# Reordering the products of the feed-forward units of a two-layer encoder trunk: g7 and g4 ahead of the down products, another opening of unit 1

## The chip, the cores and the metric

The kernel runs on one core of one Trainium2 chip. The metric is the device time of one execution in microseconds (us); lower is better. The engines are called as in the profile: PE (matrix products; PEld its weight loads), DVE (vector), ACT (scalar and activation), POOL (general purpose) and SP, which issues DMA transfers. POOL issues transfers too, among them those that add what they bring to what is in the buffer.

## What is computed

Two layers over a sequence of 512 positions with 1024 features. Layer 0 mixes the positions with a gated linear recurrence, layer 1 with stick-breaking attention; each mixer is followed by a gated feed-forward block of 2816 inner features. Everything is float32.

```python
def reference(x, norm_mix_g, norm_ffn_g, ...):
    for layer in range(DEPTH):                       # 2 layers
        h = _rmsnorm(x, norm_mix_g[layer])
        mix = _rglru_mixer(...) if layer % 2 == 0 else _sb_mixer(...)
        x = x + mix
        h = _rmsnorm(x, norm_ffn_g[layer])
        x = x + _swiglu(h, ffn_w_gate[layer], ffn_w_up[layer], ffn_w_down[layer])
    return _rmsnorm(x, final_g)

def _swiglu(h, w_gate, w_up, w_down):
    g = h @ w_gate.astype(h.dtype)
    u = h @ w_up.astype(h.dtype)
    return (jax.nn.silu(g) * u) @ w_down.astype(h.dtype)
```

The change touches the two feed-forward blocks and the final norm.

## The kernel before

**Split products.** Each float32 operand is split into a high half (`wh`, a cast on ACT) and a low half (`wl`, the difference, on DVE or POOL; line L302). A product is three matmuls: high times high, high times low, low times high (L760 to L762). So every weight block of 128x1024, called a chunk here, costs PE 12 matmuls of 512 columns, ACT one cast and DVE or POOL one subtraction.

**Units.** The 2816 inner features are worked in five full units of 512 and one half unit of 256 (`NU` = 5; units 0 to 5). A two-by-two block scheme with seven products instead of eight is used twice: for gate and up (steps g1 to g7, two chunks each in a full unit, c0 and c1) and for the down product of the previous unit (steps d1 to d7, one chunk each). Unit 0 has no down products. `tt` transposes the previous unit's activations on PE; o1 and o2 make the operands of the down products out of them on ACT and DVE; q1 and q2 multiply up by silu of gate on DVE.

**Weights of the products.** Sums of weight blocks are built up in place. g1 and g2 use raw blocks. g5 uses the sum of two blocks in a buffer `bu`: SP loads one, POOL adds the other with an accumulating transfer (L90). When g5's chunk has been split, POOL adds a third block to the same buffer, which makes g6's weights, and after g6 a fourth, which makes g4's. g3 uses a raw block in a buffer `bv`; when that has been split, POOL adds a block, which makes g7's weights. The sums of down weights are made on POOL (`minus`, L142) and DVE (`sums`, L162).

**Banks.** The eight PSUM banks are used in pairs: A, B, `db` and `tb`. In a unit, A takes g1, then g6 on top (copied out to `u2`), then g7 (added to `b5`), then g4, which after silu is gate's second half; then g2 overwrites A. B takes g5 and g3. q2 and q1 read A. The down products use `db` and `tb`, and after each one DVE adds the banks to the result rows `y`.

**What sets the order.** In the feed-forward blocks the order on PE, ACT, DVE and POOL is that of the program text: a string per unit lists the steps. A product's `chunk()` also issues the casts and subtractions of the chunk three places ahead; there are four buffers for split weights, so the cast of a chunk can run once the chunk four places ahead of it in the list has been multiplied. SP issues loads up to some ten chunks ahead. Each engine works through its list in order and waits at the first entry that is not ready.

Of the kernel before, what the change touches and what calls it, by code (L numbers as in the profile page):

```python
# [17 lines left out]
S = 512  # L18
# [14 lines left out]
NU = 5  # L33
# [11 lines left out]
class Unit:  # L45
    def __init__(self, kern, l, u):
        self.kern, self.u = kern, u
        self.w = FB if u < NU else FB // 2
        self.np = 2 if u < NU else 1
        self.kt = 2 if u < NU else 4  # L50
        self.src = kern.a["w_gu"][l, 8 * u:8 * u + 4 * self.np]
        self.down = kern.a["w_dn"][l, 4 * (u - 1):4 * u] if u else None
        self.b, self.d = {}, {}
        self.direct = u == NU
        if u == 0:
            self.order = "g1 g5 stats g2 x0 g6 x1 g3 q1 g4 x2 g7 x3"
        elif u < NU:
            self.order = "g5 g1 tt g6 o1 o2 g3 d1 d2 g7 d6 d5 g4 d7 d3 g2 d4"
        else:
            self.order = "g5 g1 tt g6 o1 g3 o2 d1 g2 d2 g7 d6 d5 g4 q2 d7 tn d3 d4"  # L60
        if u == NU - 1:
            self.order = self.order.replace("g2 d4", "g2 q1 d4")
        self.pieces = []
        for n in self.order.split():
            if n[0] not in "gd":
                continue
            q = int(n[1])
            self.pieces += [Piece(self, q, c) for c in range(self.np)] if n[0] == "g" else [DownPiece(self, q)]


class Piece:
    LOADS = {1: ("raw", 0), 2: ("raw", 2), 5: ("bu", 0), 3: ("bv", 3)}
    HOME = {1: 1, 2: 2, 5: 5, 6: 5, 4: 5, 3: 3, 7: 3}
    def __init__(self, unit, q, c):
        self.unit, self.q, self.c = unit, q, c
        self.pool = (q, c) in ((7, 1), (2, 1)) and unit.u > 0 and unit.np == 2
        self.summed = False

    def buf(self, tag, pool, bufs):
# [51 lines left out]
class DownPiece(Piece):  # L131
    def __init__(self, unit, q):
        self.unit, self.q, self.c = unit, q, 0
        self.pool = q in (5, 4)
        self.summed = False

    def ready(self):
# [6 lines left out]
    def load(self):  # L144
        un, kern = self.unit, self.unit.kern
        for k in {1: ("12", "22", "11"), 2: ("21",)}.get(self.q, ()):
            t = un.d[k] = kern.raw_buf() if k in ("11", "21") else self.buf("d" + k, kern.fp, 1)
            kern.nc.sync.dma_start(t, un.down[("11", "21", "12", "22").index(k)])
        if self.q == 1:
            un.d["t"] = self.buf("dt", kern.fp, 1)  # L150
            n = 6 if un.direct else 3
            self.minus("t", "22", "12", n)
            self.minus("12", "12", "11", n + 1)

# [14 lines left out]
class Kern:  # L169
# [318 lines left out]
    def finish(self, banks, ys, g):  # L488
# [2 lines left out]
        nc.vector.tensor_scalar(g, g, -0.5, None, ALU.mult)  # L491
        row = lambda i, lo, hi: st[:, NT * i + lo:NT * i + hi]
        sq = [self.tmp() for _ in range(2)]
        late = ((1, 1), (2, 1), (3, 1))

        def gather(t, h):
            y = ys[t][:, hs[h]]
# [5 lines left out]
        def half(t):  # L503
            nc.vector.tensor_scalar(row(2, t, t + 1), row(0, t, t + 1), 1.0 / D, EPS, ALU.mult, ALU.add)

        def root(t):
            nc.scalar.activation(row(3, t, t + 1), row(1, t, t + 1), AF.Sqrt, scale=1.0 / D, bias=row(2, t, t + 1))

        def chain(lo, hi):
            s1, v0, r, v, q = (row(i, lo, hi) for i in (1, 2, 3, 4, 5))  # L510
            nc.vector.scalar_tensor_tensor(v, s1, 1.0 / D, v0, ALU.mult, ALU.add)
            nc.vector.reciprocal(r, r)
            nc.vector.tensor_tensor(v, v, r, ALU.mult)
            nc.vector.tensor_tensor(v, v, r, ALU.mult)
            nc.vector.scalar_tensor_tensor(q, v, -3.0, r, ALU.add, ALU.mult)
# [26 lines left out]
        gather(3, 0)  # L542
        store(1, 1)
        store(0, 1)
        chain(2, 3)
        gather(3, 1)
        half(3)
        root(3)
        store(2, 1)
        store(1, 0)  # L550
        store(2, 0)
        chain(3, 4)
        store(3, 0, 2)
        store(3, 1, 2)

    def v_chunk(self, pv, c):
# [167 lines left out]
    def ffn(self, l, gnext):  # L724
# [3 lines left out]
        with tc.tile_pool(name=f"ffn{l}", bufs=1) as self.fp, \  # L728
# [67 lines left out]
            def dproduct(q, two, mid):  # L796
                wh, wl = self.chunk()
                n, first, a, d = DOWN[q]
                banks = two[n]
                for i in range(2):  # L800
                    for p in range(2):
                        mm3(banks[i], *stat(q, p, i), wh[:, ts(p, S)], wl[:, ts(p, S)], first and p == 0, p == 1)
                if mid:
                    mid()
                for i in range(2):
                    t = 2 * a + i
                    o = y[t][:, ts(d, S)]
                    if gnext and (t, d) not in started:
                        started.add((t, d))
                        nc.scalar.copy(o, banks[i])  # L810
                    else:
                        add(o, o, banks[i])
# [9 lines left out]
            for u in range(NU + 1):  # L822
                un = self.unit_of()
                w = un.w
                A, B = gb
                B2 = tb if u == 0 else B if u == NU else A
                B4 = db if u == 0 else A
                two = (tb, db) if u == NU else (db, tb)
# [107 lines left out]
                        split([t[:, p] for t in hn], A[p])  # L936

                steps = dict(q1=q1, q2=q2, g1=g1, g2=g2, g3=g3, g4=g4, g5=g5, g6=g6, g7=g7, stats=stats, tt=tt, o1=o1, o2=o2, tn=tn)
                mids = {7: q2, 4: q1} if u < NU - 1 else {7: q2} if u < NU else {2: q1}
                steps.update({f"d{q}": (lambda q=q: dproduct(q, two, mids.get(q))) for q in range(1, 8)})  # L940
                steps.update({f"x{t}": (lambda t=t: None if gnext else turned(t)) for t in range(NT)})
                for n in un.order.split():
# [440 lines left out]
```

## Time and profile before

| what | value |
|---|---|
| median of 3 runs | 1137.63 us (1136.78 to 1137.96) |
| profiled execution, its own time | 1136.93 us |
| span of the profiled execution | 1135.2 us |
| granted PE clock, mean | 0.995 |
| feed-forward units 1 to 5 of layer 0 | 206 to 493 us of the span |
| feed-forward units 1 to 5 of layer 1 | 824 to 1114 us |
| last matmul starts | 1125.03 us |

Rows of the timeline have: start in us from the span's start, duration, engine, line, operation, output and inputs, shapes, and in brackets how long the engine was idle before it and what ended that. `x2` merges two like operations in a row; the duration is then that of both. Rows of waits have: who waited for whom, us in total, times, longest. Rows of transfers have: what was issued by which queue, how many, size, median us from issue to landing. In the prediction, lines are those of the kernel before; in the change everything behind the first edit stands two lines further down.

### The profile page before, as it was taken

What the parts mean: (1) busy time and instruction counts of PE and PEld (TensorE: products, weight loads), DVE (VectorE), ACT (ScalarE), POOL (GpSimd) and SP (SyncE); (2) the same over time, 40 slices, a digit from 0 to 9 for tenths busy, and PEclk for the clock granted to TensorE, in tenths of its full rate; (3) what the DMA queues carried; (4) which work ended last, traced back from release to release, by engine and by line L of the source; (5) the groups of instructions that cost most, each with busy time, mean ns of one, the idle gap of its engine ahead of it and who ended that gap; (6) DMA issues with size and microseconds to landing.
All of it is one profiled execution on the core that took longest, in us unless ns stands there. A gap on an engine that the chain in (4) does not pass through costs nothing.

```text
span 1135.2 us, 14824 instructions
## 1 busy us (share of the span) xinstructions
PE 1098.4 (97%) x5265; PEld 908.2 (80%) x5265; DVE 893.1 (79%) x1237; ACT 708.0 (62%) x1088; POOL 415.0 (37%) x271
## 2 busy tenths in 40 slices
PE   9999999999999999899999999899999999999986
PEld 6887788788888888778888888778878887888865
DVE  7878887686969687987388898768478796969797
ACT  6598567565545464535389999868574655555454
POOL 2451232335353534214044443412135344353422
PEclk9999999999999999999999999999999999999998
DMA  8522338858485857242334333125876858584511
GB/s 284 163 79 89 111 116 218 174 159 203 139 205 126 236 113 222 64 155 81 102 103 110 96 94 92 59 93 151 200 150 182 182 159 192 154 204 115 139 48 74
DMA packets 48970, 159.87 MB, mean 141 GB/s; under 512 B 6017, under 2 KB 7553, under 8 KB 48897
## 3 DMA queue, kind: packets, MB, share of 16 engines
q1 hardware_dynamic: 36512, 113.84, 29.2%
q0 software_dynamic: 12384, 45.09, 22.5%
q8 instruction: 41, 0.67, 0.2%
q14 instruction: 33, 0.26, 0.1%
HBM read 148.43 MB, written 2.10 MB: 133 GB/s over the span
## 4 chain that ended last, share of the span: by engine, by line
PE 60%; DVE 12%; issue 7%; ACT 6%; DMA 6%; POOL 1%; SPq 0%; ACTq 0%; DVEq 0%; POOLq 0%
PE bank L761 12%; PE bank L760 12%; PE bank L762 12%; PE bank L347 6%; PE bank L349 5%; PE bank L348 5%; DMA bu<-w_gu 5%; DVE wl L302 4%; PE bank L1165 3%; ACT wh L301 2%; PE bank L1191 2%; PE bank L767 1%; DVE y L752 1%; PE bank L1110 1%; PE bank L1111 1%
## 5 line engine op out<-in xcount | busy, mean ns | idle before, releaser
L301 ACT CAST wh<-raw 128x1024 fp32r<-128x1024 f32 (+1 forms) x144 | 144.7, 1011 | 80.7 <-DVE raw L162 35.4
L760 PE MATMUL bank<-wh,ow 128*128 128x512 f32 (+1 forms) x480 | 180.2, 375 | 0.4 <-DVE u L752 0.4
L761 PE MATMUL bank<-wl,ow 128*128 128x512 f32 (+1 forms) x480 | 178.8, 372 | 0.8 <-DVE wl L302 0.8
L762 PE MATMUL bank<-wh,ow 128*128 128x512 f32 (+1 forms) x480 | 178.6, 372 | 0.0
L302 DVE TENSOR_TENSOR wl<-raw,wh 128x1024 fp32r<-128x1024 f32 (+1 forms) x110 | 142.6, 1298 | 35.9 <-ACT wh L301 34.8
L302 DVE TENSOR_TENSOR wl<-bu,wh 128x1024 fp32r<-128x1024 f32 x66 | 98.8, 1507 | 63.1 <-ACT wh L301 62.1
L90 POOL DMA_DIRECT2D bu<-w_gu x64 | 56.0, 875 | 201.0 <-DVE wl L302 140.8
L301 ACT CAST wh<-bu 128x1024 fp32r<-128x1024 f32 x66 | 69.4, 1051 | 85.6 <-DMA bu<-w_gu 55.3
L302 POOL TENSOR_TENSOR wl<-raw,wh 128x1024 fp32r<-128x1024 f32 (+1 forms) x34 | 80.1, 2355 | 115.7 <-ACT wh L301 115.7
L752 DVE TENSOR_TENSOR y<-y,bank 128x512 f32<-128x512 f32 x140 | 90.9, 679 | 18.5 <-PE bank L762 18.4
L761 PEld LDWEIGHTS bank<-wl,ow 128*128 128x128 f32 x480 | 90.5, 189 | 16.8 <-DVE wl L302 1.6
L347 PE MATMUL bank<-uh,wh 128*128 128x512 f32 x256 | 102.6, 401 | 1.4 <-DVE t L1075 0.6
L760 PEld LDWEIGHTS bank<-wh,ow 128*128 128x128 f32 x480 | 90.5, 188 | 16.8 <-DVE u L752 1.3
L762 PEld LDWEIGHTS bank<-wh,ow 128*128 128x128 f32 x480 | 90.4, 188 | 15.6
L349 PE MATMUL bank<-uh,wl 128*128 128x512 f32 x256 | 100.4, 393 | 1.4 <-DVE wl L302 1.4
L348 PE MATMUL bank<-ul,wh 128*128 128x512 f32 x256 | 99.8, 390 | 0.3 <-DVE ul L404 0.3
L761 PE MATMUL bank<-wl,hth 128*128 128x512 f32 x192 | 75.3, 392 | 3.5 <-POOL wl L302 3.1
L302 POOL TENSOR_TENSOR wl<-d,wh 128x1024 fp32r<-128x1024 f32 x20 | 50.6, 2530 | 67.7 <-ACT wh L301 67.7
L760 PE MATMUL bank<-wh,hth 128*128 128x512 f32 x192 | 75.1, 391 | 0.0
L762 PE MATMUL bank<-wh,htl 128*128 128x512 f32 x192 | 74.9, 390 | 0.0
L1133 POOL TENSOR_TENSOR spl<-t,sph 128x512 fp32r<-128x512 f32 (+1 forms) x32 | 36.3, 1157 | 85.6 <-DVE sph L1132 79.8
L459 POOL TENSOR_TENSOR acc<-acc,t 128x512 f32<-128x512 f32 x20 | 28.8, 1440 | 82.5 <-ACT t L457 75.4
(257 smaller groups left out, 2850.7 us busy)
## 6 DMA issues: line engine op xcount, KB each, us to landing
bu<-w_gu POOLq DMA_DIRECT2D x64, 512.0 KB, 6.3
raw<-w_gu SPq DMA_DIRECT2D x44, 512.0 KB, 3.5
raw<-w_dn SPq DMA_DIRECT2D x24, 512.0 KB, 6.4
bu<-w_gu SPq DMA_DIRECT2D x22, 512.0 KB, 5.5
bv<-w_gu SPq DMA_DIRECT2D x22, 512.0 KB, 3.8
bv<-w_gu POOLq DMA_DIRECT2D x22, 512.0 KB, 6.5
d<-w_dn SPq DMA_DIRECT2D x20, 512.0 KB, 5.3
raw<-w_qk SPq DMA_DIRECT2D x16, 512.0 KB, 3.5
```

Source lines behind the costliest of these rows:

```text
L90: kern.soon(lambda: kern.nc.gpsimd.dma_start(t, self.part(n), accum_op=ALU.add))
L301: self.nc.scalar.copy(wh[:, c], raw[:, c])
L302: self.wl_engine(i).tensor_tensor(wl[:, c], raw[:, c], wh[:, c].bitcast(F32), ALU.subtract)
L347: mm(out, lhsT=wh, rhs=xh, start=first, stop=False)
L348: mm(out, lhsT=wh, rhs=xl, start=False, stop=False)
L349: mm(out, lhsT=wl, rhs=xh, start=False, stop=last)
L752: add = lambda o, a, b: nc.vector.tensor_tensor(o, a, b, ALU.add)
L760: mm(out, lhsT=xh, rhs=wh, start=first, stop=False, skip_group_check=True)
L761: mm(out, lhsT=xh, rhs=wl, start=False, stop=False, skip_group_check=True)
L762: mm(out, lhsT=xl, rhs=wh, start=False, stop=last, skip_group_check=True)
L1133: nc.gpsimd.tensor_tensor(sl[:, w], sp[:, w], sh[:, w].bitcast(F32), ALU.subtract)
L1165: mm(zt[kt][:, o0:o0 + ZW[j]], lhsT=tri if j == kt else one_n, rhs=s_, start=False, stop=True, skip_group_check=True)
```

## The change

In units 1 to 4 the step string puts g7 directly behind g3, g4 behind d2 and g2 ahead of d7; d7, d3 and d4 close the unit. q2 now runs in d6 and q1 in d7 (in unit 4, q1 follows g2). Unit 1 opens with g1 instead of g5. From unit 1 on the pairs A and B are swapped. POOL takes the low halves of g7's second chunk and, in full units, of d5, d7 and d4; DVE takes that of g2's second chunk and all of unit 5's. Two subtractions on POOL are issued after one chunk instead of three. In d1 the four groups of matmuls go by weight half first. In the final norm, the row tile (3, 0) is multiplied by the gain on DVE at its store instead of on POOL, its store is one transfer instead of two, and a chain of small operations moves behind the last add.

```diff
-            self.order = "g5 g1 tt g6 o1 o2 g3 d1 d2 g7 d6 d5 g4 d7 d3 g2 d4"
+            self.order = "g5 g1 tt g6 o1 o2 g3 g7 d1 d2 g4 d6 d5 g2 d7 d3 d4"
...
         if u == NU - 1:
-            self.order = self.order.replace("g2 d4", "g2 q1 d4")
+            self.order = self.order.replace("g2 d7", "g2 q1 d7")
+        if u == 1:
+            self.order = self.order.replace("g5 g1", "g1 g5")
...
-        self.pool = (q, c) in ((7, 1), (2, 1)) and unit.u > 0 and unit.np == 2
+        self.pool = (q, c) == (7, 1) and unit.u > 0 and unit.np == 2
...
-        self.pool = q in (5, 4)
+        self.pool = q in (5, 7, 4) and not unit.direct
...
-            n = 6 if un.direct else 3
+            n = 6 if un.direct else 1
...
-        late = ((1, 1), (2, 1), (3, 1))
+        late = ((1, 1), (2, 1), (3, 0), (3, 1))
...
-        chain(2, 3)
         gather(3, 1)
         half(3)
+        chain(2, 3)
         root(3)
...
-        store(3, 0, 2)
+        store(3, 0)
...
-                for i in range(2):
-                    for p in range(2):
-                        mm3(banks[i], *stat(q, p, i), wh[:, ts(p, S)], wl[:, ts(p, S)], first and p == 0, p == 1)
+                pairs = [(i, p) for i in range(2) for p in range(2)]
+                for i, p in sorted(pairs, key=lambda e: e[1]) if q == 1 else pairs:
+                    mm3(banks[i], *stat(q, p, i), wh[:, ts(p, S)], wl[:, ts(p, S)], first and p == 0, p == 1)
...
-                A, B = gb
+                A, B = gb[::-1] if u else gb
...
-                mids = {7: q2, 4: q1} if u < NU - 1 else {7: q2} if u < NU else {2: q1}
+                mids = {6: q2, 7: q1} if u < NU - 1 else {6: q2} if u < NU else {2: q1}
```

ACT in unit 2 of layer 0, from the end of `tt`'s operand work to behind that of o2, before: `raw` of number 213 and 215 are the weights of d1 and d2, the two `bv` those of g3's second chunk (first row) and g7's two chunks (last rows).

```order
L301 CAST wh70_2378<-bv_210_2190 128x1024
L301 CAST wh71_2395<-raw213_2214 128x1024
L869 COPY u20_1495<-bank0_70 128x512
L869 COPY u21_1496<-bank1_71 128x512
L771 COPY t219_2413<-bank4_74 128x512
L756 CAST hah_1503<-t219_2413 128x256
L756 CAST hbh_1505<-bank5_75 128x512
L756 CAST hth_1507<-t220_2417 128x512
L756 CAST hth_1507<-t221_2418 128x512
L301 CAST wh472_2429<-raw215_2234 128x1024
L301 CAST wh73_2445<-bv_209_2168 128x1024
L301 CAST wh74_2465<-bv_210_2190 128x1024
```

The same place of the change:

```order
L303 CAST wh70_2378<-bv_210_2188 128x1024
L303 CAST wh71_2395<-bv_209_2170 128x1024
L871 COPY u20_1495<-bank2_72 128x512
L871 COPY u21_1496<-bank3_73 128x512
L773 COPY t220_2415<-bank4_74 128x512
L758 CAST hah_1503<-t220_2415 128x256
L758 CAST hbh_1505<-bank5_75 128x512
L758 CAST hth_1507<-t221_2419 128x512
L758 CAST hth_1507<-t222_2420 128x512
L303 CAST wh472_2431<-bv_210_2188 128x1024
L303 CAST wh73_2449<-raw213_2254 128x1024
L303 CAST wh74_2467<-raw215_2275 128x1024
```

g7's two casts stand where those of d1 and d2 stood: the first ahead of the operand work of o1 and o2, the second behind it.

DVE at the end of unit 2, before: the splits of `bu` are those of g5 of unit 3, that of `raw226` is g1 of unit 3, the adds onto `bank0` and `bank1` belong to g2, `u2` to q1, the adds onto `y` to the down products.

```order
L752 TENSOR_TENSOR y1_1500<-y1_1500,bank7_77 128x512
L302 TENSOR_TENSOR wl484_2662<-bu_224_2525,wh484_2661 128x1024
L302 TENSOR_TENSOR wl85_2686<-bu_225_2546,wh85_2685 128x1024
L752 TENSOR_TENSOR bank0_70<-r10_1493,bank0_70 128x512
L752 TENSOR_TENSOR bank1_71<-r11_1494,bank1_71 128x512
L302 TENSOR_TENSOR wl86_2709<-raw226_2548,wh86_2708 128x1024
L859 SCALAR_TENSOR_TENSOR u20_1495<-u20_1495,nrs_130,bank0_70 128x512
L859 SCALAR_TENSOR_TENSOR u21_1496<-u21_1496,nrs_130,bank1_71 128x512
L752 TENSOR_TENSOR y2_1501<-y2_1501,bank4_74 128x512
L752 TENSOR_TENSOR y3_1502<-y3_1502,bank5_75 128x512
```

The same place of the change, where `bank2` and `bank3` are A:

```order
L754 TENSOR_TENSOR bank2_72<-r10_1493,bank2_72 128x512
L754 TENSOR_TENSOR bank3_73<-r11_1494,bank3_73 128x512
L304 TENSOR_TENSOR wl484_2662<-bu_224_2505,wh484_2661 128x1024
L861 SCALAR_TENSOR_TENSOR u20_1495<-u20_1495,nrs_130,bank2_72 128x512
L861 SCALAR_TENSOR_TENSOR u21_1496<-u21_1496,nrs_130,bank3_73 128x512
L754 TENSOR_TENSOR y2_1501<-y2_1501,bank4_74 128x512
L754 TENSOR_TENSOR y3_1502<-y3_1502,bank5_75 128x512
L304 TENSOR_TENSOR wl85_2683<-bu_225_2527,wh85_2682 128x1024
L754 TENSOR_TENSOR y0_1499<-y0_1499,bank6_76 128x512
L754 TENSOR_TENSOR y1_1500<-y1_1500,bank7_77 128x512
L304 TENSOR_TENSOR wl86_2702<-raw226_2548,wh86_2701 128x1024
```

g2's adds moved ahead of both of unit 3's splits, q1 behind the first, and d7's and d3's adds onto `y` now follow q1.

POOL in the middle of unit 2, before: `bv` is g7's second chunk, `d12` the weights of d5 and later d4, `raw` g2's second chunk, `bu` of number 224 and 225 the buffers of unit 3's g5.

```order
L302 TENSOR_TENSOR wl74_2466<-bv_210_2190,wh74_2465 128x1024
L302 TENSOR_TENSOR wl476_2505<-d12_211_2210,wh476_2504 128x1024
L142 TENSOR_TENSOR d12_211_2210<-raw215_2234,raw213_2214 128x1024
L90 DMA bu_224_2525<-w_gu 128x1024
L90 DMA bu_225_2546<-w_gu 128x1024
L302 TENSOR_TENSOR wl82_2620<-raw223_2469,wh82_2619 128x1024
L302 TENSOR_TENSOR wl83_2642<-d12_211_2210,wh83_2641 128x1024
```

The same place of the change, where `dt` is the weight sum of d7:

```order
L304 TENSOR_TENSOR wl472_2432<-bv_210_2188,wh472_2431 128x1024
L92 DMA bu_224_2505<-w_gu 128x1024
L92 DMA bu_225_2527<-w_gu 128x1024
L304 TENSOR_TENSOR wl78_2545<-d12_211_2250,wh78_2544 128x1024
L144 TENSOR_TENSOR d12_211_2250<-raw215_2275,raw213_2254 128x1024
L304 TENSOR_TENSOR wl81_2604<-dt_214_2256,wh81_2603 128x1024
L304 TENSOR_TENSOR wl83_2640<-d12_211_2250,wh83_2639 128x1024
```

The two transfers for unit 3 moved ahead of d5's split.

## The prediction

> **What bounds the kernel now.** I read the busy table first, then who TensorE (PE) waited for, then the timeline of the four helper engines around one unit.
>
> ```profile
> PE 1098.4 (97%) x5265; PEld 908.2 (80%) x5265; DVE 893.1 (79%) x1237; ACT 708.0 (62%) x1088; POOL 415.0 (37%) x271
> ...
> PE bank L760 <- ACT hah L756: 4.1, 2, 2.6
> PE bank L760 <- DVE u L859: 3.3, 4, 1.6
> PE bank L761 <- POOL wl L302: 3.1, 2, 1.6
> PE bank L761 <- DVE wl L302: 3.1, 5, 1.0
> ...
> PE bank L767 <- DVE b L911: 2.3, 2, 1.2
> ```
>
> PE is busy for 97% of the span; each row behind gives the waits for one releaser: total, times, longest. The change keeps every matmul, so it can gain only what PE waits for in the feed-forward layers, plus the tail behind the last matmul. It can lose wherever a weight comes later than its product. A wait costs about 0.16 us more than its idle time, since matmuls start 0.227 us apart and are counted as 0.39 long:
>
> ```profile
> 267.81 0.39 PE L760 MATMUL bank<-wh,ow 128*128 128x512 f32 x1
> ...
> 291.35 0.39 PE L760 MATMUL bank<-wh,hah 128*128 128x512 f32 x1
> ...
> 294.06 0.39 PE L760 MATMUL bank<-wh,hbh 128*128 128x512 f32 x1
> 294.29 0.39 PE L761 MATMUL bank<-wl,hbh 128*128 128x512 f32 x1
> ```
>
> These rows are unit 2 of layer 0: its start, its d1 and its d2 (first and second matmul). A chunk of 12 matmuls takes 2.72 us, and PE did not wait once between these rows. In the new order g7 stands where d1 and d2 stand, so g7's second chunk must have its high half at 294.06 and its low half (`wl`) at 294.29, 26.48 after the unit's start. The feeders at that place, ACT and then POOL:
>
> ```profile
> 283.87 1.05 ACT L301 CAST wh<-bv 128x1024 fp32r<-128x1024 f32 x1
> 284.82 1.05 ACT L301 CAST wh<-raw 128x1024 fp32r<-128x1024 f32 x1
> ...
> 291.23 1.05 ACT L301 CAST wh<-raw 128x1024 fp32r<-128x1024 f32 x1
> 292.19 2.00 ACT L301 CAST wh<-bv 128x1024 fp32r<-128x1024 f32 x2
> ...
> 279.08 0.89 POOL L90 DMA_DIRECT2D bv<-w_gu  x1
> 286.53 0.87 POOL L90 DMA_DIRECT2D bv<-w_gu  x1 [6.56 <-DVE wl L302]
> 294.27 2.66 POOL L302 TENSOR_TENSOR wl<-bv,wh 128x1024 fp32r<-128x1024 f32 x1 [6.87 <-ACT wh L301]
> ```
>
> The casts at 283.87 (g3's second chunk) and 284.82 (d1) stand ahead of the operand work o1 and o2 on ACT, the cast at 291.23 (d2) behind it, 6.41 after the one at 284.82. The two POOL transfers at 279.08 and 286.53 add another weight block into g3's buffers and so make g7's weights. Their times to landing, one view for each (then the third transfer ahead of them, for its 5.7):
>
> ```profile
> bv<-w_gu POOLq DMA_DIRECT2D x1, 512.0 KB, 9.4
> ...
> bv<-w_gu POOLq DMA_DIRECT2D x1, 512.0 KB, 5.6
> ...
> bu<-w_gu POOLq DMA_DIRECT2D x1, 512.0 KB, 5.7
> ```
>
> So g7's first chunk was complete at 279.08 + 9.4 = 288.5 (it queued behind two others; alone it takes 5.6 to 5.7), the second at 286.53 + 5.6 = 292.1. Before, g7 was used at 296.79 and this was early enough.
>
> **The change, part by part.**
>
> *g7 directly behind g3, units 2 to 4.* The cast of g7's first chunk moves into the place of 284.82 and that of the second into the place of 291.23. First chunk: its transfer is issued when g6's and g3's splits are done. Those splits stand behind work that the new order puts ahead of the unit's start (two adds of 1.29 together and q1):
>
> ```profile
> 267.13 1.29 DVE L752 TENSOR_TENSOR bank<-r,bank 128x512 f32<-128x512 f32 x2
> ...
> 271.88 1.39 DVE L859 SCALAR_TENSOR_TENSOR u<-u,nrs,bank 128x512 f32<-128x512 f32 x2
> ...
> 275.24 2.35 DVE L302 TENSOR_TENSOR wl<-bu,wh 128x1024 fp32r<-128x1024 f32 x2
> ```
>
> I take 1.29 + 1.39 = 2.7 off: landing at 285.8, cast at 285.9, and the in-order ACT reaches the second chunk 6.41 later, at 292.3. The second chunk's own transfer hangs on the split of g3's second chunk, which does not move: 292.1. Both say 292.2. Then cast 1.05, hand-over 0.08, POOL split 2.66: 296.0, against 294.29: a wait of 1.7 in each unit. Floor: if nothing but ACT's order binds, 291.23 + 3.79 = 295.0, a wait of 0.7. Ceiling: if the first transfer still lands at 288.5, the cast is at 295.0 and the wait 4.5. I take 1.7, since two independent paths give it. Units 2 to 4 of two layers: 6 x 1.7 = 10.2. Cast and split of g7's second chunk are cover for nothing else; d1 and d2 behind it are ready.
>
> The split that decides here stays on POOL. [...]
>
> *Unit 1 opened by g1, banks swapped.* What it removes:
>
> ```profile
> 203.54 1.05 ACT L301 CAST wh<-bu 128x1024 fp32r<-128x1024 f32 x1 [5.86 <-DMA bu<-w_gu]
> ...
> 204.62 1.22 DVE L302 TENSOR_TENSOR wl<-bu,wh 128x1024 fp32r<-128x1024 f32 x1 [5.69 <-ACT wh L301]
> 213.35 1.40 DVE L911 SCALAR_TENSOR_TENSOR b<-b,nrs,bank 128x512 f32<-128x512 f32 x2
> ...
> 205.97 0.39 PE L760 MATMUL bank<-wh,ow 128*128 128x512 f32 x1
> 209.97 0.50 PE L761 MATMUL bank<-wl,ow 128*128 128x512 f32 x1 [0.76 <-DVE wl L302]
> 212.99 0.47 PE L760 MATMUL bank<-wh,a 128*128 128x512 f32 x1 [0.22 <-ACT bank L887]
> 217.17 0.50 PE L761 MATMUL bank<-wl,a 128*128 128x512 f32 x1 [0.95 <-DVE wl L302]
> ```
>
> ACT stood for 5.86 us behind g5's late transfer, and PE paid three waits, 2.7 us by the distances of matmul starts (1.9 in layer 1). g1 needs no transfer of that kind and g5 comes 5.44 later: I take all 4.6 as gained. The swap keeps the first product on banks 2 and 3, which were free, so it costs nothing. But g6's weights are g5's plus a transfer, and now there are two chunks between them, not four. Unit 1 starts at 205.97. g5's first split at 204.6 to 205.8, four adds (2 x 1.28), q2 (1.40), second split 1.22: 211.0. Transfer 5.7: 216.8. Cast 1.05, split 1.22: 219.2. Next transfer 5.7: 225.0. g3's transfer is issued at 220.5 behind it: alone it lands at 226.1, with as much queueing as in the 9.4 above at 229.9; the one ahead of it is nearly through, so I take 227.5. g7's first chunk is cast at 227.6, the second 6.41 later at 234.0, its split ends at 234.0 + 3.79 = 237.8. PE wants it at 205.97 + 26.48 = 232.45: 5.3. Layer 1 in the same way: 4.7. Together 10.0, with 7.2 as the floor (g3's transfers unqueued, 1.4 less each) and 14.8 if it lands as late as before.
>
> *q1 early, d7 d3 d4 last.* q1's four waits go: 3.3 idle plus 4 x 0.16, about 4.1 with one refill, gained, since d3, d4 and g5 now lie between q1 and the g1 that overwrites its bank. Late next: d4 writes the banks that d7's evacuation still reads, and that evacuation stands on DVE behind g5's first split and q1. The silu between them:
>
> ```profile
> 267.85 1.26 ACT L855 ACTIVATE bank<-bank,rsT 128x512 f32<-128x512 f32 x2 [1.90 <-DVE bank L752]
> ```
>
> From the end of g2: hand-over 0.2, add 0.65, silu 0.65, cast 1.05, split 1.23, q1 1.39, first add 0.69 make 5.8; d4 comes after 5.44. With the refill 0.45 in units 1 to 3: 2.7 (0 to 5). Next-unit g5 weights are loaded two chunks earlier and don't bind there.
>
> *POOL's other work.* d7 goes to POOL, g2's second chunk to DVE. POOL now issues the next unit's two transfers ahead of d5's split; each waits for a load that follows g4's splits. d5 then has about 1 us to spare once PE has waited at g7. I cost it at 0 (0 to +4 over both layers). The two subtractions come out two chunks earlier in the program but still behind the same transfers on POOL: 0.
>
> *Unit 5.* d5's split goes from POOL to DVE:
>
> ```profile
> 474.34 1.28 DVE L752 TENSOR_TENSOR y<-y,bank 128x512 f32<-128x512 f32 x2
> 475.82 2.55 DVE L302 TENSOR_TENSOR wl<-bu,wh 128x1024 fp32r<-128x1024 f32 x1 [0.21 <-ACT wh L301]
> ...
> 474.93 2.36 POOL L302 TENSOR_TENSOR wl<-d,wh 128x1024 fp32r<-128x1024 f32 x1 [19.73 <-ACT wh L301]
> ...
> 477.35 0.51 PE L761 MATMUL bank<-wl,hth 128*128 128x512 f32 x1 [1.58 <-POOL wl L302]
> ```
>
> On DVE it ends near 475.6 + 1.22 = 476.8 instead of 477.3: 0.45 a layer. In d1, ordering by weight half moves the late operand three matmuls, 0.68, and DVE is relieved of q1 at the unit's start; of 4.1 waited there I take 2.1. Together 3.0 (1 to 5.5).
>
> *Tail.* POOL no longer multiplies the last row tile's first half, and a DVE chain moves behind the last add:
>
> ```profile
> 1125.62 1.26 POOL L501 TENSOR_TENSOR y<-y,raw 128x512 f32<-128x512 f32 x1 [1.43 <-ACT t L499]
> ...
> 1125.63 1.27 DVE L513 TENSOR_TENSOR st<-st 128x1 f32<-128x1 f32 x1
> ...
> 1127.20 0.68 DVE L498 TENSOR_TENSOR y<-y,bank 128x512 f32<-128x512 f32 x1
> 1128.88 2.12 ACT L523 ACTIVATE y<-y,st 128x512 f32<-128x512 f32 x4
> ```
>
> A 128x1 operation that takes 0.16 elsewhere took 1.27 beside POOL's, and held up the last add. That add can now come at about 1125.5; the results are ready at about 1130.4 instead of 1131.0, and the stores queue less: 1.5 gained (0.4 to 2). [...]
>
> Sum: +10.2 +10.0 +2.7 -4.6 -4.1 -3.0 -1.5 = +9.7. The profiled execution took 1136.93 (span 1135.2), 0.70 under the median 1137.63; 1136.93 + 9.7 = 1146.6, as a median 1147.3; I say 1147.
>
> **The rivals.** (1) Faster: g7 waits only for ACT's order. It needs both accumulating transfers to land by 291.2, that is the second 0.9 sooner. Then 6 x 0.7 + 7.2 - 4.6 - 4.1 - 5.5 - 2 = -4.8: 1133. For it: POOL is otherwise idle there. Against it: the split that releases the second transfer sits behind tt's operand work, unmoved. It decides where the mean wait at g7 is under about 1.6. (2) A wash: the g7 wait is 1.0 in units 2 to 4, unit 1's at its floor and d4's nil: 6.0 + 7.2 - 13.2, about 1137.5. (3) Much slower: the transfers land as late as before: 6 x 4.5 + 14.8 + 2.7 - 13.2 = +31, 1169. Against it: DVE is relieved at the unit's start.
>
> **How the numbers follow.** Forecast 0.69, (1) 0.13, (2) 0.10, (3) 0.08. Less than 0.2% (2.3 us) is about what a measurement here can't tell from no change. Slower 0.69 + 0.08 = 0.77, same 0.10, faster 0.13. The forecast's own range is 1140 to 1156: waits of 1.2 to 2.4 at g7, 4 to 6 in unit 1, 0 to 5 at d4. The range 1135 to 1157 adds the wash and half of (1), and leaves out the rest of (1), most of (3) and the upper edge.
>
> **What would show it.** In the changed profile PE's waits for POOL's `wl` should grow from 3.1 in two to about 20 in eight to ten, all at g7's second chunk, the longest in unit 1; its waits for q1 (`u`, 3.3) should be gone; ACT should stand still for a `bv` transfer ahead of o1, which it did not before; d4's first matmul should wait for a DVE add on `y` up to 0.5 in units 1 to 3; the last store should be issued about 1.5 sooner after the last matmul. No POOL wait at g7 would make the prediction wrong as a whole.

## The result, and the profile after

The changed kernel took 1168.83 us (median; 1167.37 to 1172.12) against 1137.20 us of the kernel before in the same session: 1.0286 times as long, with an interval of 1.0259 to 1.0313. It is slower, as forecast, but by 32 us and not by 10; the forecast range (1135 to 1157) does not hold it. Its profiled execution took 1172.12 us with a span of 1170.4 us, 35.2 us longer than that of before. The medians of the kernel before lie between 1131.03 and 1137.20 us on the chips used, so experiments below are compared by their ratio to the kernel before on the same chip.

The busy table of the changed kernel:

```profile
PE 1114.0 (95%) x5265; PEld 916.6 (78%) x5265; DVE 911.0 (78%) x1242; ACT 711.3 (61%) x1086; POOL 400.0 (34%) x266
```

PE has the same 5265 matmuls, but is counted busy for 15.6 us longer: matmuls themselves have become slower somewhere. Its waits (who waited for whom, us in total, times, longest):

```profile
PE bank L763 <- POOL wl L304: 15.4, 8, 1.9
PE bank L762 <- ACT wh L303: 10.7, 8, 2.3
PE bank L762 <- DVE y L754: 5.8, 8, 2.1
...
PE bank L762 <- DVE u L754: 1.8, 2, 0.9
...
PE bank L762 <- ACT hah L758: 1.3, 2, 0.7
...
PE bank L762 <- DVE b L913: 0.6, 2, 0.4
...
PE bank L769 <- DVE b L913: 0.6, 2, 0.3
```

The first row is the split of g7's second chunk on POOL, once in each of units 1 to 4 of both layers; the second is for the most part the cast of the same chunk. The waits for q1 (`u`, L861 now) are gone. The place in unit 4 of layer 0, on PE (the last four rows are in d1, which follows g7's second chunk):

```profile
429.64 0.50 PE L762 MATMUL bank<-wh,s 128*128 128x512 f32 x1 [2.20 <-ACT wh L303]
432.08 0.80 PE L763 MATMUL bank<-wl,s 128*128 128x512 f32 x1 [1.94 <-POOL wl L304]
432.67 0.63 PE L764 MATMUL bank<-wh,s 128*128 128x512 f32 x1
433.10 0.63 PE L762 MATMUL bank<-wh,s 128*128 128x512 f32 x1
...
437.36 0.56 PE L763 MATMUL bank<-wl,hah 128*128 128x512 f32 x1
437.76 0.39 PE L764 MATMUL bank<-wh,hal 128*128 128x512 f32 x1
437.99 0.39 PE L762 MATMUL bank<-wh,hah 128*128 128x512 f32 x1
438.22 0.40 PE L763 MATMUL bank<-wl,hah 128*128 128x512 f32 x1
```

PE stands for 2.2 us for the high half, runs one matmul, stands for 1.94 us for the low half, and then the matmuls start 0.43 us apart instead of 0.227 until 437.8. The view by stretches names the reason (stretch, length, then busy time and count of PE, PEld, DVE, ACT and POOL, the granted PE clock, DMA share, GB/s):

```profile
432.00:437.90 5.90, 5.82 (x14) 4.65 (x15) 5.86 (x7) 1.10 (x2) 0.02 (x1) 0.52 0.31 101
437.90:443.80 5.90, 5.90 (x28) 4.86 (x27) 5.50 (x7) 2.20 (x3) 0.88 (x1) 1.00 0.71 196
```

At a clock of 0.52, 14 matmuls run in the time that 28 take at 1.00. This stretch alone costs 2.7 us on top of the waits.

How much longer each unit got, from the starts of its first matmul and of the next unit's in the two profiles, in us:

| layer | unit 1 | unit 2 | unit 3 | unit 4 | unit 5 |
|---|---|---|---|---|---|
| 0 | +5.9 | +3.8 | +5.0 | +7.2 | -0.6 |
| 1 | +5.1 | +3.0 | +3.5 | +5.5 | -2.5 |

Why the chunk comes late, in unit 3 of layer 0 (its first matmul starts at 336.41), on ACT, POOL and DVE:

```profile
344.77 1.05 ACT L303 CAST wh<-bv 128x1024 fp32r<-128x1024 f32 x1 [1.66 <-PE bank L764]
...
356.63 1.05 ACT L303 CAST wh<-bv 128x1024 fp32r<-128x1024 f32 x1 [3.10 <-DMA bv<-w_gu]
...
363.05 1.04 ACT L303 CAST wh<-bv 128x1024 fp32r<-128x1024 f32 x1
...
344.91 1.88 POOL L92 DMA_DIRECT2D bu<-w_gu  x2 [2.71 <-DVE wl L304]
347.44 0.88 POOL L92 DMA_DIRECT2D bv<-w_gu  x1 [0.65 <-DVE wl L304]
...
364.18 2.35 POOL L304 TENSOR_TENSOR wl<-bv,wh 128x1024 fp32r<-128x1024 f32 x1 [8.16 <-ACT wh L303]
...
345.86 1.23 DVE L304 TENSOR_TENSOR wl<-bv,wh 128x1024 fp32r<-128x1024 f32 x1 [0.30 <-ACT wh L303]
```

The chain: the cast of g3's first chunk (344.77) waits for PE to free a buffer; its split on DVE (the last row) stands 0.30 us for that cast and then lets POOL issue the transfer at 347.44, 11.03 us after the unit's start, behind two transfers issued at 344.9 and 345.9. ACT stands 3.10 us for it, until 356.6, 9.1 us after its issue. The cast of g7's second chunk follows 6.42 us later, behind the operand work of o1 and o2, and POOL's split ends at 366.5. PE needed it 26.48 after the unit's start, at 362.9; with the 1.5 us that PE had waited for the cast it lost 3.7 us there and 1.4 more at the low clock.

### The profile page after: what moved, and what is told of

Read it like the earlier page. It is cut to its first block, busy times and chain, and to the rows that moved or that the text cites. A ratio compares the mean times of both kernels' runs of the same rounds, so it can differ in the third digit from the quotient of the medians.

```text
span 1170.4 us, 14792 instructions
## 1 busy us (share of the span) xinstructions
PE 1114.0 (95%) x5265; PEld 916.6 (78%) x5265; DVE 911.0 (78%) x1242; ACT 711.3 (61%) x1086; POOL 400.0 (34%) x266
## 5 line engine op out<-in xcount | busy, mean ns | idle before, releaser
L304 DVE TENSOR_TENSOR wl<-raw,wh 128x1024 fp32r<-128x1024 f32 (+1 forms) x118 | 197.7, 1679 | 59.6 <-ACT wh L303 59.1
L304 DVE TENSOR_TENSOR wl<-bu,wh 128x1024 fp32r<-128x1024 f32 x66 | 82.0, 1249 | 32.2 <-ACT wh L303 31.2
L763 PEld LDWEIGHTS bank<-wl,ow 128*128 128x128 f32 x480 | 90.5, 188 | 15.4
L304 POOL TENSOR_TENSOR wl<-raw,wh 128x1024 fp32r<-128x1024 f32 (+1 forms) x26 | 59.2, 2278 | 111.9 <-ACT wh L303 111.9
L304 DVE TENSOR_TENSOR wl<-bv,wh 128x1024 fp32r<-128x1024 f32 x36 | 49.2, 1366 | 30.8 <-ACT wh L303 29.8
L303 ACT CAST wh<-bv 128x1024 fp32r<-128x1024 f32 x44 | 46.2, 1051 | 40.2 <-DMA bv<-w_gu 29.3
```

Source lines behind the costliest of these rows:

```text
L303: self.nc.scalar.copy(wh[:, c], raw[:, c])
L304: self.wl_engine(i).tensor_tensor(wl[:, c], raw[:, c], wh[:, c].bitcast(F32), ALU.subtract)
L763: mm(out, lhsT=xh, rhs=wl, start=False, stop=False, skip_group_check=True)
```

## The experiments

Unless it is said otherwise, each kernel is the changed kernel with the edit shown, and waits are PE's. "Measured" gives the time as a ratio to the kernel before on the same chip, with the 95% interval in brackets.

**1. The old order with the other edits kept.**

```diff
-            self.order = "g5 g1 tt g6 o1 o2 g3 g7 d1 d2 g4 d6 d5 g2 d7 d3 d4"
+            self.order = "g5 g1 tt g6 o1 o2 g3 d1 d2 g7 d6 d5 g4 d7 d3 g2 d4"
-                mids = {6: q2, 7: q1} ...
+                mids = {7: q2, 4: q1} ...
```

> The changed kernel with the step order of before in units 1 to 4 (g3 d1 d2 g7 d6 d5 g4 d7 d3 g2 d4); the opening of unit 1, the swapped banks, the POOL splits, the d1 order and the tail stay changed. Theory A (all of the loss is g7 standing directly behind g3): the waits at g7 go, and what remains are the gains: unit 1's opening 4.6, unit 5 about 2, tail 1.4, so about 1137 - 8 = 1129. Rival B (the swapped banks or the other POOL splits cost as well): it stays above 1137.

Measured: 1.0367 [1.0351, 1.0383]. The waits moved rather than went:

```profile
PE bank L763 <- POOL wl L304: 30.9, 8, 5.4
```

They are no longer at g7 but at d7, one a unit: in the old order d7's split on POOL stands behind the next unit's two transfers, which POOL can't issue until their loads are in. So this run mixed two causes, and experiment 5 parts them.

**2. The operands of o1 and o2 behind g3.** ACT then reaches g7's casts with the operand work not between them.

```diff
-            self.order = "g5 g1 tt g6 o1 o2 g3 g7 d1 d2 g4 d6 d5 g2 d7 d3 d4"
+            self.order = "g5 g1 tt g6 g3 o1 o2 g7 d1 d2 g4 d6 d5 g2 d7 d3 d4"
```

> The changed kernel with o1 and o2 moved behind g3, so that ACT casts g7's second chunk ahead of o2's operand work and not behind it. Theory A (ACT's order adds 6.41 us between g7's two casts): the cast comes as soon as the transfer lands, 24.3 after the unit's start, only the POOL split of 2.3 to 2.7 is left to wait for, about 1.7 a unit in units 2 to 4 and no slow stretch behind it: about 1168.8 - 20 = 1148. Rival B (the second chunk's own transfer is the late one): no change beyond 3 us.

Measured: 1.051 [1.0476, 1.0545]. In units 2 to 4 the wait at g7 fell to 1.2 to 1.4 us, all of it POOL's split, so ACT's order does carry the larger part of it. But the time was lost again behind it:

```profile
PE bank L762 <- DVE b L913: 13.7, 8, 2.3
PE bank L763 <- POOL wl L304: 10.5, 8, 1.9
PE bank L762 <- DVE hbl L753: 7.8, 7, 1.1
...
PE bank L762 <- DVE t L753: 4.0, 7, 0.6
```

d1 now waits twice, once for each of its two banks, until DVE's operand work (`t`, `hbl`) has read what `tt` left there, and g2 waits for q2 (`b`). The theory was right on the wait and wrong on the total.

**3. POOL's two subtractions eight chunks late instead of one.**

```diff
-            n = 6 if un.direct else 1
+            n = 6 if un.direct else 8
```

> The changed kernel with the two subtractions of down weights on POOL issued eight chunks late instead of one, behind g7's transfers and split. Theory A (at the unit's start these subtractions hold up DVE's splits of two SBUF inputs, so the chain of accumulating transfers starts about 2.5 late): g7's first transfer lands near 16.5 instead of 20 after the unit's start, the wait in units 2 to 4 falls from 4.8 to about 1.7, in all -10 to -20 (some waits come back at g4, where the subtractions then stand): about 1153. Rival B (the transfers queue for themselves): under 4 us.

Measured: 1.0457 [1.0429, 1.0486]. In unit 3 of layer 0 (start 341.16), POOL and ACT:

```profile
346.88 0.86 POOL L92 DMA_DIRECT2D bu<-w_gu  x1 [5.75 <-DVE wl L304]
349.47 0.86 POOL L92 DMA_DIRECT2D bu<-w_gu  x1 [1.73 <-DVE wl L304]
352.18 0.88 POOL L92 DMA_DIRECT2D bv<-w_gu  x1 [1.85 <-DVE wl L304]
...
359.18 1.05 ACT L303 CAST wh<-bv 128x1024 fp32r<-128x1024 f32 x1 [0.91 <-PE bank L763]
365.60 1.05 ACT L303 CAST wh<-bv 128x1024 fp32r<-128x1024 f32 x1
```

The transfer of `bv` is issued at 11.02, as before, but now the two ahead of it were issued earlier (5.7 and 8.3 after the unit's start instead of 8.5 and 9.5), and it has landed by 18.0 instead of 20.2. The second cast is again 6.42 later, and PE waits 1.6 us at g7: the forecast's own sum for a landing at 18.0 was 1.7. So it is in units 3 and 4 of both layers, where the first transfer lands at 17.7 to 18.3 and PE waits 1.4 to 1.9 us for POOL's split. In unit 2 the split is 2.1 and 2.3 us late: in layer 0 the second transfer landed later (at 24.95 instead of 24.2), in layer 1 the first one (at 19.1); slow matmuls follow in both. This shows the transfers queueing behind each other, and what POOL's subtractions have to do with it. That the total is worse has another cause, again a wait of g2 for q2 (`b`), 13.3 us in eight. The subtractions now run beside DVE's splits in the unit's middle: in unit 2 of layer 0 two of these take 2.20 and 3.42 us, where the changed kernel has 1.21 for each, and q2 starts 50.2 us after the unit's start instead of 47.5.

**4. The split of g7's second chunk on DVE.**

```diff
-        self.pool = (q, c) == (7, 1) and unit.u > 0 and unit.np == 2
+        self.pool = False
```

> The changed kernel with the low half of g7's second chunk on DVE instead of POOL. Theory A: the split ends 1.1 to 1.4 sooner in each of 8 units (9 to 11), and where the wait falls under about 3 us the slow matmuls behind it go too (another 2 to 6): about 1155. Rival B (DVE is busy there): no gain.

Measured: 1.0254 [1.0232, 1.0276].

```profile
PE bank L762 <- ACT wh L303: 9.4, 7, 2.4
PE bank L763 <- DVE wl L304: 7.1, 12, 0.8
```

The wait between cast and split fell from 2.21 to 1.03 us of matmul distance in all eight places, as DVE takes 1.2 us where POOL takes 2.4; 9.4 us in sum and 4 us less of slow matmuls. The casts came as late as before. So POOL's slowness is some 13 us of the loss between these two profiles, and not the root of it. In time less of it arrives: against the ratios of the changed kernel (1.0286, and 1.0321 in experiment 9, both on other chips), 1.0254 is 4 to 8 us less.

**5. Old order and the old split assignment; kept are unit 1's opening, the swapped banks, unit 5 on DVE, d1's order and the tail.**

```diff
 (as in 1, and)
-        self.pool = (q, c) == (7, 1) and unit.u > 0 and unit.np == 2
+        self.pool = (q, c) in ((7, 1), (2, 1)) and unit.u > 0 and unit.np == 2
-        self.pool = q in (5, 7, 4) and not unit.direct
+        self.pool = q in (5, 4) and not unit.direct
-            n = 6 if un.direct else 1
+            n = 6 if un.direct else 3
```

> The changed kernel with the step order of units 1 to 4 and the split assignment of full units as before (g7's and g2's second chunks, d5 and d4 on POOL, d7 on DVE); kept are unit 1's opening with the swapped banks, unit 5 on DVE, d1 by weight half, the new tail. Theory A (the loss is all in g7's early place; d7 on POOL is harmless there, but was the fault in the run with the old order alone): those parts gain what the trace of the changed kernel showed, 3 to 4.6 in unit 1, 2 to 3 in unit 5, 1.4 in the tail: 0.992 to 0.995 of before, and the 30.9 us that the run with the old order waited for POOL's splits falls under 5. Rival B (unit 1's opening, the swap or unit 5 on DVE cost more than they gain): 1.00 to 1.02.

Measured: 0.9986 [0.9973, 1.0000]. The whole loss is gone, so order and split assignment of units 1 to 4 hold it. The kept parts, however, gain 1.6 us and not the 6 to 9 expected. By place: the tail is 1.4 shorter; unit 1 of layer 0 still waits 0.9, 1.2 and 1.3 us, at other places than before and not less in sum; in unit 5 d5 waits 2.2 us for a bank that DVE has yet to empty in place of 1.7 for POOL's split, and in both layers about 1.5 us of slow matmuls follow.

**6. The new order with the old split assignment** (the last three edits of 5 alone).

> The changed kernel, with only the split assignment of full units as before (g2's second chunk on POOL, d7 on DVE, the two subtractions three chunks late). Theory A: the waits at g7's second chunk come from its place in the order, so they stay: POOL's and the cast's waits together 22 to 30 us, 1.02 to 1.035 of before. Rival B (the work moved to POOL is what delays g7): those waits fall under 12 and the time is 1.005 to 1.015 of before.

Measured: 1.0365 [1.0349, 1.0380]. The waits at g7 stay. The order makes the loss, not what was moved to POOL; with experiment 1, d7 on POOL costs that much only together with the old order.

**7. Only g7 moved, in the kernel before.**

```diff
-            self.order = "g5 g1 tt g6 o1 o2 g3 d1 d2 g7 d6 d5 g4 d7 d3 g2 d4"
+            self.order = "g5 g1 tt g6 o1 o2 g3 g7 d1 d2 d6 d5 g4 d7 d3 g2 d4"
```

> The kernel before with one step moved: in units 1 to 4 g7 stands directly behind g3, ahead of d1 and d2; everything else as before. Theory A (g7's early place alone makes the loss; its second chunk hangs on two accumulating transfers that cannot come 5.4 us sooner): 4 to 8 us in each of units 1 to 4 of both layers, 25 to 40 us in all, 1.022 to 1.035 of before, nearly all of it waits at g7's second chunk and slow matmuls behind them. Rival C (the loss comes from g7's place together with the new end of the unit, whose work on DVE and POOL delays the transfers): under 14 us, below 1.012.

Measured: 1.0447 [1.0402, 1.0491], above what theory A expected.

```profile
PE bank L761 <- POOL wl L302: 18.3, 10, 1.9
PE bank L760 <- ACT wh L301: 12.0, 10, 2.0
```

The same two waits, of which eight each are g7's, and 4.1 to 8.1 us a unit. One moved step is enough for the whole loss; the other edits of the change take some 14 us of it back (1.0447 against 1.0321 for the changed kernel on the same chip, experiment 9).

**8. The changed kernel with g7 one product later.**

```diff
-            self.order = "g5 g1 tt g6 o1 o2 g3 g7 d1 d2 g4 d6 d5 g2 d7 d3 d4"
+            self.order = "g5 g1 tt g6 o1 o2 g3 d1 g7 d2 g4 d6 d5 g2 d7 d3 d4"
```

> The changed kernel with g7 one product later, between d1 and d2 (2.72 us), its two casts then both behind o2's operand work. Theory A (a fixed ready time of g7's second chunk against a moved deadline): each unit's wait at g7 shrinks by 2.5 to 2.7, to 0 to 2.5 in units 2 to 4 and 2 to 5 in unit 1; with idles that short few slow matmuls behind them. Total 8 to 18 us over before, 1.007 to 1.016. Rival D (the transfers are late because POOL and DVE are busy in the new order, and slip with it): the waits stay at 3 to 6 a unit, 1.025 or more.

Measured: 1.0048 [1.0032, 1.0064], below what either theory expected. Unit 3 of layer 0 (start 330.45) on POOL, ACT and PE:

```profile
341.48 0.88 POOL L92 DMA_DIRECT2D bv<-w_gu  x1 [0.58 <-DVE wl L304]
...
355.96 2.49 POOL L304 TENSOR_TENSOR wl<-bv,wh 128x1024 fp32r<-128x1024 f32 x1 [5.91 <-ACT wh L303]
...
353.88 2.00 ACT L303 CAST wh<-bv 128x1024 fp32r<-128x1024 f32 x2
...
359.67 0.39 PE L763 MATMUL bank<-wl,s 128*128 128x512 f32 x1
```

The transfer is issued at 11.03 again. But both casts of g7 now stand behind the operand work, back to back, POOL's split ends at 358.45, and the product that needs it starts at 359.67 without a wait. There is no wait for POOL left in the list of waits. A place 2.72 us later is worth 31 us over eight units (1.0321 - 1.0048 = 0.0273 of 1133.2), 3.9 a unit: at most 2.7 of it can be the later deadline by itself; the rest goes with ACT's order and with the clock, which no longer drops there (the matmuls around that start are 0.23 us apart, and the mean clock of the profiled execution is 0.994, against 0.982 for the changed kernel). No run parts these.

**9. The changed kernel again, on the chip of 7, 8 and 11.**

> The changed kernel itself, unaltered, on the chip of the kernels beside it, since the kernel before differs by 6 us between chips. All theories: slower than before by 30 to 40 us, 1.026 to 1.036.

Measured: 1.0321 [1.0290, 1.0352].

**10. Work for PE while it stands.** Between g7's two chunks, 22 matmuls of 256 columns whose result nobody reads.

```diff
+                        if q == 7 and c == 1 and u:
+                            oh = self.ops[0][q][0]
+                            for _ in range(22):
+                                mm(tb[0][:, :HS], lhsT=oh[:, ts(0)], rhs=oh, start=True, stop=True, skip_group_check=True)
```

> The changed kernel with 22 matmuls of 256 columns, whose result nobody reads, between g7's two chunks in units 1 to 4, about 2.5 us of work where PE stood idle. Theory A (after an idle of some 3.3 us or more the next matmuls start 0.43 us apart, not 0.227, and that is about a third of the loss): the slow stretches shrink from 19 us in 108 matmuls to under 10, with the waits themselves as long as before (less what the fillers cover): 1.015 to 1.022 of before. Rival (the matmuls are slow because they wait for their operands, not for the clock): the slow stretches stay and the time is 1.028 or more.

Measured: 1.0345 [1.0324, 1.0366], on the chip of experiment 9: no gain, against theory A's forecast. Yet the matmuls did as it said. The same stretch of unit 4:

```profile
432.00:438.00 6.00, 5.77 (x26) 4.60 (x25) 6.00 (x7) 1.82 (x2) 0.42 (x1) 1.00 0.27 88
```

Clock 1.00, where it was 0.52. In units 1 to 4 the excess of slow matmuls fell from 12 us to 4. What ate the gain is in the trace: the fillers take 2.6 us in each of eight places, but in unit 2 PE had waited only about 0.3 us for the cast, so there they mostly delay, and the wait for POOL's split comes behind them as before. Useless work in the idle kept the clock at 1.00 here, but where it was longer than the idle it cost time.

**11. g4 and g2 one product earlier, g7 in its old place,** on the kernel before, with the tail, d1's order and unit 5's splits taken from the change.

```diff
-            self.order = "g5 g1 tt g6 o1 o2 g3 d1 d2 g7 d6 d5 g4 d7 d3 g2 d4"
+            self.order = "g5 g1 tt g6 o1 o2 g3 d1 d2 g7 d6 g4 d5 d7 g2 d3 d4"
-                mids = {7: q2, 4: q1} ...
+                mids = {5: q2, 3: q1} ...
```

> The kernel before with g7 in its old place, and only the parts that paid kept: the new tail, d1 by weight half, unit 5's splits on DVE; banks, unit 1's opening and POOL's splits in full units as before; the unit's end reordered so that q1 has two products between itself and the next unit: g7 d6 g4 d5 d7 g2 d3 d4, q2 in d5, q1 in d3. Theory A: the tail 1.4, q1's waits 4.1 and about 3 in unit 5 are gained, d4 pays up to 2.7: 4 to 8 us under before, 0.993 to 0.997. Rival E (DVE has no idle time between g7 and d7, so q2 comes late and g2 waits for it, as with g2 one product earlier): 2 to 6 us at g2 in each of units 1 to 3, 1.01 to 1.03.

Measured: 1.0086 [1.0065, 1.0107]; both theories missed. q1's waits are gone and g2 does not wait, but d5's split on POOL is late for its product by 1.3 to 1.9 us in units 1 to 3 of both layers (besides, a cast at the opening of unit 1 in layer 0 came 2.2 us late):

```profile
PE bank L761 <- POOL wl L302: 8.4, 6, 1.8
```

**12. g2 one product earlier, otherwise as in 5** (order ending "g4 d7 g2 d3 d4", q2 in d7, q1 in d3).

> The old order and old split assignment as in the kernel beside it, but g2 one product earlier: d7 g2 d3 d4 at the unit's end, q1 in d3. Theory A: the waits of the next unit's g1 for q1 (4.1 us in the kernel before) go, and d4's waits of 0.45 in six units (2.7) come or not: 0 to 4 us less than the kernel with g2 in its old place, 0.988 to 0.994 of before. Rival: g2's product then waits for q2 on DVE, as the late-operand kernels did: 3 to 6 us more than that kernel, 0.996 to 1.000.

Measured: 1.0251 [1.0204, 1.0298], with times scattered from 1150.9 to 1180.3 us; the ratio is that of the three shortest, and the profile is of the longest, so its waits are larger than the ratio's. The rival had it, but far too small.

```profile
PE bank L762 <- DVE b L913: 37.7, 8, 6.3
```

g2 overwrites the bank that q2 reads, q2 stands in d7 directly ahead of it, and DVE reaches q2 some 6 us late. It is not that DVE has no idle time, as the expectation before had it for its rival. In unit 1 of layer 0, DVE and POOL:

```profile
254.58 6.50 DVE L304 TENSOR_TENSOR wl<-d,wh 128x1024 fp32r<-128x1024 f32 x1 [4.31 <-ACT wh L303]
261.00 1.39 DVE L913 SCALAR_TENSOR_TENSOR b<-b,nrs,bank 128x512 f32<-128x512 f32 x2
...
255.03 2.67 POOL L304 TENSOR_TENSOR wl<-raw,wh 128x1024 fp32r<-128x1024 f32 x1
257.34 2.65 POOL L304 TENSOR_TENSOR wl<-d,wh 128x1024 fp32r<-128x1024 f32 x1
```

DVE stands 4.31 us for a cast, and the split ahead of q2 then takes 6.50 us instead of 1.2, beside two splits on POOL, and ends 1.09 after the second.

**13 and 14. The parts that stood for gains, alone on the kernel before:** the tail, and the tail with d1 by weight half and unit 5's splits on DVE.

> The kernel before with the new tail of the final norm alone. Theory F (the tail's 1.4 us between the last matmul and the end, the same in every profile of a kernel that has it, is a gain by itself): 1.4 us less, 0.9980 to 0.9995. Rival G (the tail is paid back earlier or is lost in the scatter): 0.9995 to 1.0005.

> The kernel before with the new tail, d1 by weight half and unit 5's splits on DVE. The prediction's terms: 1.5 + 3.0 = 4.5 us, 0.996. Theory F (unit 5's DVE split only exchanges the 1.7 us wait for POOL's split and a 1.3 us wait behind it for one of 2.2 us for a bank, behind which PE's clock drops in about half the cases, some 1.5 us): no more than 1 us lower than the tail alone, 0.9975 to 0.9995.

Measured: 0.9991 [0.9975, 1.0007] and 0.9986 [0.9967, 1.0005]. In both profiles the last matmul starts 8.8 us before the end, as in every kernel with the new tail, against 10.2 before. Whether 1 us of 1131 is a gain in time these intervals don't settle; the medians give unit 5's edits another 0.6 us, which is far inside the intervals. These two and experiment 5 are the fastest kernels found, and none of them is clearly faster than the kernel before. The tail's profile also shows, on another chip, waits of the old code that the forecast had counted as there to be gained:

```profile
PE bank L760 <- ACT hah L756: 0.4, 2, 0.3
...
PE bank L760 <- DVE u L859: 0.3, 1, 0.3
```

They read 4.1 and 3.3 in the profile of before, and nothing at these places is changed in this kernel. Unit 1's opening, also unchanged here, still waits: 4.5 us in layer 0 and 1.3 in layer 1.

## Why the prediction was right in sign and wrong in size

The excess of matmul starts over 0.227 us, summed by step over units 1 to 5 of both layers, changed kernel less kernel before, against the terms of the sum:

| term | predicted | in the two profiles |
|---|---|---|
| g7, waits in units 2 to 4 | +10.2 | +20.6 |
| g7, waits in unit 1 | +10.0 | +10.2 |
| slow matmuls behind these waits, in g7 and d1 | none | +12.4 |
| d4's banks | +2.7 | +3.3 |
| unit 1's opening | -4.6 | -5.2 |
| q1 before g1 | -4.1 | -4.6 |
| unit 5 | -3.0 | -2.1 |
| g2 waiting for q2 in unit 2 | none | +1.2 |
| tail | -1.5 | -1.4 |
| sum | +9.7 | +34.4 (spans: +35.2) |

The row of unit 5 holds -0.4 in the matmuls of its steps and -1.7 in the wait of the closing transposes for q2, which the rows of waits for `b` show (L767 before, 2.3 us idle in two, in the prediction; L769 after, 0.6 in two). Of the rest of the spans, 0.9 lies between the two feed-forward blocks.

*The step that failed: "I take 1.29 + 1.39 = 2.7 off: landing at 285.8".* It took DVE's work at the unit's start for all that holds the transfer of g3's first buffer. The row of before that I had not read is the cast ahead of its split, on ACT (the second row is the split, on DVE):

```profile
276.16 1.05 ACT L301 CAST wh<-bv 128x1024 fp32r<-128x1024 f32 x1 [1.62 <-PE bank L762]
...
277.51 1.21 DVE L302 TENSOR_TENSOR wl<-bv,wh 128x1024 fp32r<-128x1024 f32 x1
```

The cast waits for PE to free one of the four buffers of split weights and ends at 277.21, only 0.3 us before the split starts. Taking work off DVE can therefore move the issue by 0.24 us in this unit (11.27 after the unit's start before, 11.03 in units 2 to 4 of both layers after), not by 2.7. Experiment 3 shows it: DVE gets there up to 2.8 us sooner, and the issue stays at 11.03.

The transfer also queues behind the two for `bu`, and in this unit these came only 0.7 us sooner (8.3 and 9.6 after its start instead of 9.0 and 10.3). q1 did leave the unit's start, but DVE's two splits beside POOL's subtractions took 6.98 us together, where they took 1.85 and 2.11 before; the forecast had put the earlier place of these subtractions at 0. So in units 2 to 4 the first transfer landed 19.0 to 21.0 us after the unit's start, where the forecast had 18.0 and the kernel before 20.7 to 22.3. Added up over the six units it is 11.4 us later than forecast, and the waits there are 10.4 us longer than forecast. Experiment 3, where the landing in units 3 and 4 is at about 18.0, has the wait that the forecast worked out for it, so the steps behind that one hold: ACT in order, 6.42 us from cast to cast, then POOL.

Rival (3) gave 1169, and the median is 1168.83. That agreement is luck. Its condition, "the transfers land as late as before", held only in part; it counted 41.8 us of waits at g7 and nothing behind them, and the profile has 30.8 us of waits and 12.4 of slow matmuls.

*"A wait costs about 0.16 us more than its idle time" is too cheap behind long waits.* Where PE stood for 2 us and more, its clock fell in part of the cases to about half (0.52 in the stretch above) for 5 to 13 matmuls. The 16 profiles of these kernels have 216 waits of PE in units 1 to 5 (each the excess of a start over 0.227 us, from 0.5 us on; those within 6 us of the first are added to it). At least five matmuls at 0.38 to 0.48 us from start to start stand among the 19 behind them as follows: under 2 us in 0 of 87, 2 to 2.5 us in 28 of 65, 2.5 to 3.5 us in 19 of 33, above 3.5 us in 29 of 31. In the changed kernel this made 12 us, a third of the loss; the profile of the kernel before has one wait above 2 us (2.7 in d1 of unit 5, with no drop behind it), so it could not show it. In the changed kernel's profile the two waits at g7's second chunk come to 3.3 to 4.7 us in six of the eight places, each with such matmuls behind it, and four waits of 2.2 us have none. The limits of about 3 and 3.3 us in the expectations of experiments 4 and 10 are estimates that agree with these; the 28 cases between 2 and 2.5 us lie below them. The same wait of 2.2 us at d5 has no drop behind it in the two layers of the changed kernel and slow matmuls in both of experiment 5. No run shows what decides between the two.

*Unit 1's and d4's terms* came out within 0.6 us, unit 1's by the chain that the forecast followed: in layer 0 its transfers for g6, g4 and g3 landed within 1 us of their forecast times. *The openings and q1's waits* were gained in this pair of profiles as forecast. For q1, the tail's profile shows that the credit belongs in the main to the one execution that was read: the old code on another chip has 0.3 us of these waits. The opening's waits are there too, but in experiment 5 the new opening waits no less in layer 0. *Unit 5* gained 2.1 instead of 3.0, and came that near by other parts than the forecast's: d1's wait shrank by 2.8 and the closing transposes' by 1.7, which was not forecast, while g2 waits 1.05 in each layer for DVE's `u` (0.36 before) and d5 2.2 for a bank in place of 1.7 for POOL. *The tail* was right: the operation of 128x1 that took 1.27 us beside POOL's now takes 0.16 with nothing on POOL beside it, and the last add starts 0.43 us after the last matmul does, where it was 2.17. No run shows what held that operation up. *What would show it:* POOL's waits were forecast at about 20 us in eight to ten at g7's second chunk and read 15.4 in eight; ACT's wait for `bv`, q1's missing waits, d4's wait of about 0.5 and the store 1.4 sooner are there. The longest g7 wait was not in unit 1 alone, but as long in unit 4.

Rival (1) is refuted: it needed both transfers by 291.2, that is 23.4 us after the unit's start, and in units 2 to 4 the second landed at 24.2 to 24.4 and the mean wait at g7 is 3.4 us. That g7's place is the cause is shown by experiments 7 and 8 from both sides: moving it alone gives the loss, moving it one product back takes nearly all of it away.

## What to carry to other kernels

Before taking time off a chain, read what releases each link of it in the row itself, a cast's bracket included; the engine with the most work ahead of a link need not be the one that holds it. When a step is moved ahead, set its deadline against the last of its feeders, and price a wait of more than 2 us with the clock that can fall behind it (to 0.52 here; slow matmuls stood behind 76 of the 129 waits of 2 us and more), not with its length alone. Credit a removed wait only as far as it stands in more than one execution of the old kernel.

## What the hardware showed that I had not expected

PE's clock fell to 0.52, and its matmuls slowed to 0.43 us from start to start (the stretch above); such slow matmuls stood behind waits that total 2 to 2.5 us in 28 of 65 cases. The slow matmuls behind a wait cost 1.0 to 2.7 us, at most about as much as the wait itself. A transfer of 512 KB that adds to its buffer landed 5.4 to 5.7 us after its issue when alone (g7's second chunk, units 2 to 4 of the changed kernel), and 8.0 to 10.0 us when two others were issued 1 to 3 us ahead of it (its first chunk there). A split on DVE beside a subtraction on POOL took three times its usual time at the start of unit 3:

```profile
336.30 3.64 DVE L304 TENSOR_TENSOR wl<-raw,wh 128x1024 fp32r<-128x1024 f32 x1
...
336.11 2.73 POOL L144 TENSOR_TENSOR dt<-d,d 128x1024 f32<-128x1024 f32 x1
```

Alone it took 1.2 us. The split ends at 339.94, 1.1 us after the subtraction beside it (338.84). The 16 profiles bear it out. In units 1 to 5 the 1853 DVE splits of 128x1024 with no tensor operation on POOL beside them took 1.20 to 1.23 us each; of the 777 that had one, 579 took more than 1.4 and up to 6.50 us, and 340 of these ended 1.1 us after POOL's operation. DVE's adds of 128x512 onto `y`, which read a bank, took 0.67 to 0.69 us beside POOL and alone (profiles of before, after and experiment 12). In experiment 3 the subtractions stand elsewhere and the transfers that hang on these splits come up to 2.8 us sooner.
